# Splitting the mixer's weights during the first feed-forward of an encoder block, with both parts kept in DRAM

## The chip, the cores and the metric

The kernel runs on one core of a Trainium2 chip. The metric is the device time of one execution in microseconds (us); the time of a kernel is the median of several runs.

## What is computed

One encoder layer on 512 tokens of width 1024, in fp32, made of three sub-layers. Each one normalizes, modulates with a shift and a scale that come from a condition vector `c`, and adds its gated result to `x`:

```python
mod = (jax.nn.silu(c) @ w_ada[l] + b_ada[l]).reshape(B, N_MOD, D)
m = [mod[:, j] for j in range(N_MOD)]

h = modulate(rmsnorm(x, ffn1_pre_g[l]), m[0], m[1])
y = swiglu(h, ffn1_w_gate[l], ffn1_w_up[l], ffn1_w_down[l])
x = x + 0.5 * m[2][:, None, :] * rmsnorm(y, ffn1_post_g[l])

h = modulate(rmsnorm(x, mix_pre_g[l]), m[3], m[4])
proj = h @ w_in[l]
...
attn = dsa_attention(q, k, v, q_idx, k_idx, w_idx, rel_bias)
lru = rg_lru_branch(x_lru, g_lru, ...)
merged = jnp.concatenate([rmsnorm(attn, attn_out_g[l]), rmsnorm(lru, lru_out_g[l])], axis=-1)
y = merged @ w_out[l]
x = x + m[5][:, None, :] * rmsnorm(y, mix_post_g[l])
...
```

The third sub-layer is a feed-forward like the first. The hidden width of both is 2816. The mixer (the second sub-layer) projects `h` to queries, keys and values, to an indexer's queries, keys and weights, and to the recurrent branch's input and gate. The indexer scores all admissible keys of a query and keeps the best 128; attention runs over these alone. A gated linear recurrence runs beside it.

## The kernel before

**The product in three.** A weight is used in two parts: `hi`, the weight rounded to the matmul's fast fp32 form (`fp32r`), and `lo`, what is left over. The activations are split in the same way (`hhi`, `hlo`, and `ahi`, `alo` for the hidden layer). `product` (lines 261 to 269) does three matmuls for each of the (mostly 8) blocks of 128 input rows: hi by hi (L267), hi by the activation's lo (L268), lo by hi (L269). A weight piece is 128x1024 (512 KB, for 128 output columns) and takes 24 such matmuls of 512 tokens, or of 256 where the tokens are done in two halves.

**Weights.** The program is a list of items (`Item`), each with the weight pieces (`Load`) that it uses and an estimate of its time on TensorE (PE). `feed_dma` (L195) issues the next raw pieces on SP's queue into 3 raw buffers. `split` (L203) takes a place in a ring of 6 split pieces, makes `hi` by an ACT copy (L207) and `lo` by a subtraction (L209) on VectorE (DVE) or GpSimd (POOL), as the `Load` says. `feed` splits up to 4 pieces ahead of the item that runs. Pieces whose tokens are done in halves (`halves`, L244) keep 5 of the split pieces for the second half and load and split the others again. So the mixer's 33 pieces (21 of `w_in`, 4 of the value weights, 8 of `w_out`) are split 41 times, 14 of them with `lo` on DVE and 27 on POOL.

**Beside the items** run background tasks, which take a step when their share of the items' estimated time has passed (`tick`, L164). In the first feed-forward that is `mod_task` (L434): 14 groups of 512 modulation columns. Two 1 MB tiles of `w_ada` a group are loaded (`wa`, L443), DVE sums them over the input rows in 8 operations (`macc`, L429 and L431), and PE turns the sums into columns with four transposes (L465). DVE's and PE's queues are executed in order, so a transpose whose `macc` is late stops PE.

**The boundary** (L375) between two sub-layers adds the result to `X`, sums squares, and makes the next `h`; for each half of the tokens it is a chain through DVE, ACT, POOL and PE, which runs beside the products of the other half.

**The mixer** (L770 on) runs as items: ten pieces in token halves (`EARLY`), then whole pieces and attention steps in the order of the list `ORDER`. In the background DVE computes the indexer's scores (`scores`, L1020, sums at L1035), the best 128 by 16 rounds of MAX8 and MATCH_REPLACE8 (`top`, L1039, L1047 and L1048), and the recurrence (L1052 on; L1076, L1077, L1104, L1106, L1124, L1127). The tile `keys` is read by the score matmuls (L1027, L1028); the biases of attention (`bring`, L1150) are loaded into its place.

**Order.** A scheduler orders the instructions of ACT, DVE, POOL and PE by an estimate of the run at build time, PE at the start by hand. SP's DMA queue follows the program as written. `X`, the layer's input, is loaded at the start and stays in two blocks (`x0`, `x1`) until the boundary.

Of the kernel before, what the change touches and what calls it, by code (L numbers as in the profile page):

```python
# [2 lines left out]

F32 = mybir.dt.float32
F32R = mybir.dt.float32r
# [24 lines left out]

NSTART = 3
NHALF = 12

UNITS = [(i, g) for g in range(4) for i in range(2)] + [(i, g) for i in range(2, 4) for g in range(4)]

# [32 lines left out]
class Load:  # L68


    def __init__(self, src, shape, lo):
        self.src, self.shape, self.lo_eng = src, shape, lo
        self.uses = 0
        self.raw = self.hi = self.lo = None


class Item:
# [24 lines left out]
class Build:  # L102
    def __init__(self, tc, pools, ins, out):
        self.tc, self.nc = tc, tc.nc
        (self.const, self.blkp, self.ring, self.work, self.small, self.psum, self.dram) = pools
        self.i = ins
        self.out = out
        self.items = []
        self.bg = []
        self.pending = {}  # L110
        self.turn = 0
        self.mixed = False
        self.btemps = self.early = None


    def blk(self, name, slot, dtype=F32, shape=(P, 4, S)):
# [78 lines left out]
    def feed_dma(self):  # L195
        while self.nd < len(self.order) and self.waiting < RAW:
            l = self.order[self.nd]
            l.raw = self.ring.tile([P] + list(l.shape), F32, name="raw", tag="raw", bufs=RAW)
            self.nc.sync.dma_start(l.raw, l.src)
            self.nd += 1  # L200
            self.waiting += 1

    def split(self, l):  # L203
        nc = self.nc
        l.hi = self.ring.tile([P] + list(l.shape), F32R, name="hi", tag="hi", bufs=RING)
        l.lo = self.ring.tile([P] + list(l.shape), F32R, name="lo", tag="lo", bufs=RING)
        nc.scalar.activation(l.hi, l.raw, AF.Copy)  # L207
        eng = nc.gpsimd if l.lo_eng == "pool" else nc.vector
        eng.tensor_tensor(l.lo, l.raw, l.hi.bitcast(F32), op=ALU.subtract)  # L209
        self.alive += 1  # L210
        self.waiting -= 1
# [9 lines left out]
    def run(self):  # L221
        self.order, pos = [], {}
        for it in self.items:
            for l in it.loads:
                if id(l) not in pos:
                    pos[id(l)] = len(self.order)
                    self.order.append(l)
        self.nd = self.ns = self.alive = self.waiting = 0
        done = 0
        for it in self.items:  # L230
            if it.loads:
                done = max([done] + [pos[id(l)] for l in it.loads])
                self.feed(done + AHEAD)
            it.fn(*it.loads)
            for l in it.loads:
                l.uses -= 1
                if l.uses == 0:
                    self.alive -= 1
            self.tick(it.us)

    def add(self, us, fn, *loads):
        self.items.append(Item(us, fn, *loads))
# [417 lines left out]
    def ffn(self, w, a, gamma, beta, first):  # L660
# [10 lines left out]
        def gate_up(f, f0):  # L671
            def one(j):
                def fn(l):
                    new_act(f0)
                    ps = self.mm()
                    self.product(ps, l, self.h, FULL, range(8))
                    state[j] = ps
                    if j == 1:
                        self.act_tile(f - f0, state[0], state[1], FULL)
                return fn  # L680
            for j in range(2):
                lo = "pool" if first and f0 == 0 and j else "dve"
                self.add(5.2, one(j), Load(gu[f - (NSTART if first else 0), j], (8, P), lo))

        def gate_up_half(f, j, f0):
            def fn(l, half, tok):
# [20 lines left out]
        for t, (f0, f1) in enumerate(THIRDS):  # L707
            nf = f1 - f0
            fs = range(f0, f1)
            if t == 0 and first:  # L710
                def st():
                    new_act(0)
                    self.start()
                    self.add_bg(self.mod_task(), 0.75)
                    if self.early:
                        with self.tc.issue_after(self.late.ins):
                            self.early()
# [11 lines left out]
                    down(t, d, nf)  # L729
            else:  # L730
                def evac(ps, d, k, half, tok, st):
                    nc.vector.tensor_tensor(self.Y[d][:, tok], self.Y[d][:, tok], ps[:, :256], op=ALU.add)
                    self.square_one(st, k, self.Y[d][:, tok], nc.vector if k >= 6 else nc.gpsimd)
                    nc.scalar.activation(self.Y[d][:, tok], self.Y[d][:, tok], AF.Copy, scale=a()[:, d:d + 1])
# [42 lines left out]
class Mixer:  # L777
# [11 lines left out]
    def plan(self):  # L789
# [5 lines left out]
        names += [("k", j) for j in range(4)] + [("q", j) for j in range(4)]  # L795
        index = {n: k for k, n in enumerate(names)}

        def load(n, lo="pool"):
            return Load(win[index[n]], (8, P), lo)


        def half_piece(n):
            def fn(l, half, tok):
                if n == EARLY[0] and half == 0:
# [2 lines left out]
                b.product(ps[:, :256], l, b.h, tok, range(8))  # L807
                self.evac(n, ps[:, :256], half, tok)
            return fn
        first_half, second_half = b.halves(lambda k: load(EARLY[k], ("dve", "pool")[k % 2]),  # L810
                                           [half_piece(n) for n in EARLY], 2.6, "h")
        b.items += first_half + second_half

        def whole(n, bank=None):
# [2 lines left out]
                b.product(ps, l, b.h, FULL, range(8))  # L817
                self.evac(n, ps, 1, FULL)
            b.add(5.2, fn, load(n))
        wvs = [Load(wv[j], (2, S), "pool") for j in range(4)]  # L820

        def value_piece(t):
            def fn(*ls):
# [28 lines left out]

        def y(half):
            return lambda e: self.y[half][:, 2 * e:2 * e + 2]
        first_half, second_half = b.last_products(
            lambda d: Load(b.i["wout"][d], (8, P), ("dve", "pool")[d % 2]), lambda: self.mg,
            (range(4, 8), range(4)), 2.6, evac, y,
            lambda: b.m(5), lambda: b.m(7), lambda: b.m(6), ("a3", "a1", "w1", "x1"), key="mg", bank=("wo", "mm"))
        def unit(k):
# [504 lines left out]
```

## Time and profile before

| | us |
|---|---|
| median of 3 runs | 1103.34 |
| lowest, highest | 1098.99, 1109.67 |
| the profiled execution, its own time | 1096.75 |
| its span, first to last instruction | 1095.0 |
| PE busy | 1046.9 (96%) |
| DVE busy | 661.6 (60%) |
| ACT busy | 455.0 (42%) |
| POOL busy | 221.7 (20%) |

A matmul counts as busy while it waits in the pipeline too, so PE's 96% isn't PE at its peak. PEld is the weight loading, which lies beside the matmuls. PEclk is the granted clock of TensorE, 1.00 for 2.4 GHz and 0.50 for 1.2 GHz. In time, the first feed-forward lies at 60 to 410 us, the mixer at 410 to 690, the second feed-forward after that.

### The profile page before, as it was taken

How to read it: one execution, taken by the hardware profiler on the slowest of the kernel's cores; microseconds unless marked ns; L12 is line 12 of the kernel's file. 1: busy time of each engine (PE TensorE's matmuls, PEld its weight loads, DVE VectorE, ACT ScalarE, POOL GpSimd, SP SyncE). 2: the span in 40 equal slices, each digit the busy share in tenths (PEclk: the TensorE clock that was granted, in tenths of full speed). 3: DMA queues.
4: the chain of work that ended last, by engine and by line, in shares of the span. 5: the costliest groups of instructions: out<-in, count | busy, mean ns of one | idle time of the engine just before them, and what ended most of it. 6: DMA issues, size and time to landing. Idle time of an engine off the chain costs nothing.

```text
span 1095.0 us, 14915 instructions
## 1 busy us (share of the span) xinstructions
PE 1046.9 (96%) x5798; PEld 880.8 (80%) x5798; DVE 661.6 (60%) x1077; ACT 455.0 (42%) x752; POOL 221.7 (20%) x178
## 2 busy tenths in 40 slices
PE   8999999999999979999899999699999999999995
PEld 7688878888888979987576669599988888888894
DVE  5598789733333378799998575995432333333434
ACT  5552222322222465654666574554332222222352
POOL 0020000000001365551323342755000000000232
PEclk9999999999999989999999999799999999999997
DMA  9577778533333263440323351333433323333312
GB/s 366 223 282 279 278 291 315 205 92 116 97 96 97 78 206 124 163 131 19 116 82 121 98 173 45 118 113 100 154 96 116 92 85 94 116 96 97 97 40 77
DMA packets 43014, 152.80 MB, mean 140 GB/s; under 512 B 5160, under 2 KB 10536, under 8 KB 38336
## 3 DMA queue, kind: packets, MB, share of 16 engines
q1 hardware_dynamic: 40656, 145.46, 39.3%
q0 software_dynamic: 2288, 6.40, 1.8%
q8 instruction: 45, 0.74, 0.3%
q14 instruction: 25, 0.20, 0.1%
HBM read 147.62 MB, written 6.31 MB: 141 GB/s over the span
## 4 chain that ended last, share of the span: by engine, by line
PE 71%; DVE 19%; issue 3%; DMA 3%; ACT 2%; SPq 0%; POOL 0%; DVEq 0%; ACTq 0%; POOLq 0%
PE mm L268 14%; PE mm L267 14%; PE mm L269 14%; PE wo L268 7%; PE wo L269 7%; PE wo L267 7%; DVE idx L1048 2%; DVE lo L209 2%; DVE m L1047 2%; DMA wa<-in_wa_dram 2%; DVE idx L1035 2%; PE mm L1176 2%; PE mm L647 1%; PE aux L1213 1%; DVE arena L1106 1%
## 5 line engine op out<-in xcount | busy, mean ns | idle before, releaser
L207 ACT ACTIVATE hi<-raw 128x1024 fp32r<-128x1024 f32 (+2 forms) x192 | 197.7, 1031 | 418.8 <-PE mm L268 161.1
L209 POOL TENSOR_TENSOR lo<-raw,hi 128x1024 fp32r<-128x1024 f32 x50 | 123.7, 2474 | 740.4 <-ACT hi L207 680.3
L209 DVE TENSOR_TENSOR lo<-raw,hi 128x1024 fp32r<-128x1024 f32 (+2 forms) x142 | 169.1, 1192 | 149.6 <-ACT hi L207 148.3
L267 PE MATMUL mm<-hhi,hi 128*128 128x512 f32 (+1 forms) x600 | 211.0, 353 | 2.0 <-ACT hhi L335 1.8
L268 PE MATMUL mm<-hlo,hi 128*128 128x512 f32 (+1 forms) x600 | 210.1, 351 | 0.8 <-DVE hlo L345 0.8
L269 PE MATMUL mm<-hhi,lo 128*128 128x512 f32 (+1 forms) x600 | 209.6, 350 | 0.0
L267 PE MATMUL wo<-hhi,hi 128*128 128x512 f32 (+1 forms) x400 | 146.5, 366 | 1.7 <-ACT arena L932 1.7
L269 PE MATMUL wo<-hhi,lo 128*128 128x512 f32 (+1 forms) x400 | 144.7, 362 | 2.1 <-POOL lo L209 2.1
L268 PE MATMUL wo<-hlo,hi 128*128 128x512 f32 (+1 forms) x400 | 144.2, 360 | 0.0
L267 PEld LDWEIGHTS mm<-hhi,hi 128*128 128x128 f32 x600 | 115.0, 192 | 18.3 <-ACT hhi L335 3.0
L268 PEld LDWEIGHTS mm<-hlo,hi 128*128 128x128 f32 x600 | 114.4, 191 | 16.0 <-DVE hlo L345 1.9
L269 PEld LDWEIGHTS mm<-hhi,lo 128*128 128x128 f32 x600 | 114.5, 191 | 14.9 <-issue 0.5
L268 PE MATMUL mm<-alo,hi 128*128 128x256 f32 (+1 forms) x330 | 109.8, 333 | 0.0
L267 PE MATMUL mm<-ahi,hi 128*128 128x256 f32 (+1 forms) x330 | 109.7, 333 | 0.0
L269 PE MATMUL mm<-ahi,lo 128*128 128x256 f32 (+1 forms) x330 | 109.7, 333 | 0.0
L267 PEld LDWEIGHTS wo<-hhi,hi 128*128 128x128 f32 x400 | 76.8, 192 | 14.3 <-ACT arena L932 2.1
L269 PEld LDWEIGHTS wo<-hhi,lo 128*128 128x128 f32 x400 | 76.2, 191 | 14.1 <-POOL lo L209 2.6
L268 PEld LDWEIGHTS wo<-hlo,hi 128*128 128x128 f32 x400 | 76.3, 191 | 11.7 <-issue 1.0
L431 DVE SCALAR_TENSOR_TENSOR macc<-wa,cs,macc 128x512 f32<-128x512 f32 x98 | 74.8, 764 | 10.2 <-DMA wa<-in_wa_dram 8.9
L268 PEld LDWEIGHTS mm<-alo,hi 128*128 128x128 f32 x330 | 62.7, 190 | 6.1
L269 PEld LDWEIGHTS mm<-ahi,lo 128*128 128x128 f32 x330 | 62.7, 190 | 5.9
L267 PEld LDWEIGHTS mm<-ahi,hi 128*128 128x128 f32 x330 | 62.5, 190 | 6.0
(258 smaller groups left out, 1617.5 us busy)
## 6 DMA issues: line engine op xcount, KB each, us to landing
raw<-in_gu_dram SPq DMA_DIRECT2D x89, 512.0 KB, 3.5
wa<-in_wa_dram SPq DMA_DIRECT2D x36, 1024.0 KB, 6.0
raw<-in_dn_dram SPq DMA_DIRECT2D x32, 448.0 KB, 3.4
raw<-in_win_dram SPq DMA_DIRECT2D x26, 512.0 KB, 3.6
raw<-in_dn_dram SPq DMA_DIRECT2D x22, 512.0 KB, 3.5
raw<-in_wout_dram SPq DMA_DIRECT2D x11, 512.0 KB, 3.9
raw<-in_w_dram SPq DMA_DIRECT2D x8, 384.0 KB, 10.2
X<-in_x_dram SPq DMA_DIRECT2D x4, 512.0 KB, 6.1
```

The costliest lines, as they stand in the source:

```text
L207: nc.scalar.activation(l.hi, l.raw, AF.Copy)
L209: eng.tensor_tensor(l.lo, l.raw, l.hi.bitcast(F32), op=ALU.subtract)
L267: self.nc.tensor.matmul(ps, l.hi[:, kt], xh[kt][:, tok], start=(q == 0), stop=False)
L268: self.nc.tensor.matmul(ps, l.hi[:, kt], xl[kt][:, tok], start=False, stop=False)
L269: self.nc.tensor.matmul(ps, l.lo[:, kt], xh[kt][:, tok], start=False, stop=(q == n - 1))
L431: nc.vector.scalar_tensor_tensor(acc, w[:, k], ck, acc, op0=ALU.mult, op1=ALU.add)
L647: self.nc.tensor.matmul(ps, w[:, j], x[k], start=(k == 0 and part == 0), stop=(k == ND - 1 and part == 2))
L1035: nc.vector.scalar_tensor_tensor(sc, rl[:, :n], w, sc, op0=ALU.mult, op1=ALU.add)
L1047: nc.vector.max(out=m8, in_=src)
L1048: nc.vector.match_replace(out=wk, in_to_replace=m8, in_values=src, imm_value=NEG)
L1106: nc.vector.scalar_tensor_tensor(xc[:, t:], x[:, :S - t], b.col("convw", 4 * (3 - t) + j), xc[:, t:], op0=ALU.mult, op1=ALU.add)
L1176: nc.tensor.matmul(ps[:, :n], self.q[rows, g, i * P:(i + 1) * P], self.k[rows, g, :n], start=True, stop=False)
```

## The change

A new class `Pre` stands for a piece that is split once, ahead of time. `pre` gives each of the 33 mixer pieces two DRAM tiles, and a background task `presplit` does the splits during the first feed-forward, one about every 7.4 us of the items' estimated time. It works in the blocks `x0` and `x1`, whose input has been used by then: it loads a raw piece, forms `hi` beside it on ACT, overwrites the raw piece with `lo` on DVE, and stores both to DRAM. All its DMAs are on POOL's queue (33 loads, 66 stores). When it has ended, `X` is loaded again from the input in DRAM. The task is run to its end before the first half-token result of the last products of the first feed-forward.

A `Load` that has a `Pre` skips the raw buffers and the split: `split` takes the place in the ring and issues two 512 KB DMAs on SP's queue, one for each part (82 in all, for 41 places). Four low parts at the beginning of the first feed-forward, which POOL formed, go to DVE.

```diff
@@ class Load / Pre
+    def __init__(self, src, shape, lo, pre=None):
+        self.src, self.shape, self.lo_eng, self.pre = src, shape, lo, pre
...
@@ feed_dma
             l = self.order[self.nd]
+            if l.pre:
+                self.nd += 1
+                continue
@@ split
+        if l.pre:
+            for t, part in zip((l.hi, l.lo), l.pre.parts):
+                nc.sync.dma_start(t.bitcast(F32), part)
+            self.alive += 1
+            return
@@ new
+    def pre(self, src, shape):
+        return Pre(src, shape, [self.dram.tile([P] + list(shape), F32, name=f"pre{next(self.count)}") for _ in range(2)])
+
+    def presplit(self):
+        nc = self.nc
+        at = {}
+        def fetch(k):
+            if k < len(self.pres):
+                t = at[k] = self.blk("pre", XS[k % 2], shape=[P, 2] + list(self.pres[k].shape))
+                nc.gpsimd.dma_start(t[:, 0], self.pres[k].src)
+        fetch(0)
+        fetch(1)
+        yield PACE
+        for k, p in enumerate(self.pres):
+            t = at.pop(k)
+            raw, hi = t[:, 0], t[:, 1].bitcast(F32R)
+            nc.scalar.activation(hi, raw, AF.Copy)
+            nc.vector.tensor_tensor(raw.bitcast(F32R), raw, t[:, 1], op=ALU.subtract)
+            nc.gpsimd.dma_start(p.parts[0], t[:, 1])
+            nc.gpsimd.dma_start(p.parts[1], raw)
+            fetch(k + 2)
+            yield PACE
+        self.X = self.big("X", XS)
+        for q in range(4):
+            nc.gpsimd.dma_start(self.X.tiles[q // 2][:, 2 * (q % 2):2 * (q % 2) + 2], self.i["x"][:, 2 * q:2 * q + 2])
@@ gate_up (first feed-forward)
-                lo = "pool" if first and f0 == 0 and j else "dve"
-                self.add(5.2, one(j), Load(gu[f - (NSTART if first else 0), j], (8, P), lo))
+                self.add(5.2, one(j), Load(gu[f - (NSTART if first else 0), j], (8, P), "dve"))
@@ start item, and first result of the last products
                     self.add_bg(self.mod_task(), 0.75)
+                    self.presplit_ = self.add_bg(self.presplit())
...
+                    if k == half == 0 and first:
+                        self.drain(self.presplit_)
@@ mixer
+        pres = {n: b.pre(win[k], (8, P)) for n, k in index.items()}
...
-        wvs = [Load(wv[j], (2, S), "pool") for j in range(4)]
+        wvs = [Load(wv[j], (2, S), None, b.pre(wv[j], (2, S))) for j in range(4)]
```

**DVE in the first feed-forward.** One group of modulation sums before, from its first operation to that of the next group: two weight pieces (`lo`) are split between the sums, and the columns of the group ahead are reduced (`modc`).

```order
L429 TENSOR_SCALAR macc<-wa,cs 128x512
L431 SCALAR_TENSOR_TENSOR macc<-wa,cs,macc 128x512 x2
L209 TENSOR_TENSOR lo<-raw,hi 128x1024
L431 SCALAR_TENSOR_TENSOR macc<-wa,cs,macc 128x512 x2
L466 TENSOR_REDUCE modc<-aux 128x4
L431 SCALAR_TENSOR_TENSOR macc<-wa,cs,macc 128x512 x2
L655 TENSOR_TENSOR a<-wo,sg 128x512
L431 SCALAR_TENSOR_TENSOR macc<-wa,cs,macc 128x512
L209 TENSOR_TENSOR lo<-raw,hi 128x1024
L658 TENSOR_TENSOR alo_1319<-a,ahi_1317 128x512
```

A group of the changed kernel. L480 and L482 are the sums, L230 is the low part, and L283 is a presplit piece.

```order
L480 TENSOR_SCALAR macc<-wa,cs 128x512
L709 TENSOR_TENSOR alo_1449<-a,ahi_1447 128x512
L525 TENSOR_TENSOR modc<-modc,cols 128x8
L482 SCALAR_TENSOR_TENSOR macc<-wa,cs,macc 128x512 x5
L230 TENSOR_TENSOR lo<-raw,hi 128x1024
L482 SCALAR_TENSOR_TENSOR macc<-wa,cs,macc 128x512
L230 TENSOR_TENSOR lo<-raw,hi 128x1024
L482 SCALAR_TENSOR_TENSOR macc<-wa,cs,macc 128x512
L283 TENSOR_TENSOR pre<-pre 128x1024
L706 TENSOR_TENSOR a<-mm,sg 128x512
```

Each group now has one presplit piece (two in one of them). On PE the last group's transposes stand behind 712 products of `product` where they stood behind 608, the first group's behind 98 where they stood behind 72.

**POOL in the mixer.** Before, between the boundary's `h` and the first scaled attention weights (`lgs`), and behind these:

```order
L336 TENSOR_SCALAR h_3627<-u,modc 128x256 x2
L209 TENSOR_TENSOR lo<-raw,hi 128x1024 x12
L1185 TENSOR_SCALAR lgs<-lgs,mx 128x128 x2
L1185 TENSOR_SCALAR lgs<-lgs,mx 128x256 x2
L209 TENSOR_TENSOR lo<-raw,hi 128x1024 x6
```

The same place now (L387 is the boundary's `h`, L1241 the scaling, L899 the load of `X` from its copy in DRAM):

```order
L387 TENSOR_SCALAR h_3875<-u,modc 128x256 x2
L1241 TENSOR_SCALAR lgs<-lgs,mx 128x128 x2
L1241 TENSOR_SCALAR lgs<-lgs,mx 128x256 x2
L899 DMA X_5698<-xd 128x4x256 x2
L1241 TENSOR_SCALAR lgs<-lgs,mx 128x128 x2
```

The 18 subtractions are gone from this stretch of POOL's queue.

**SP's queue around the first bias loads.** Before, the raw data of ten projection pieces, of the four value pieces (`wv`) and of three further projection pieces, then the biases:

```order
L199 DMA raw<-in_win_dram 128x1024 x10
L199 DMA raw<-in_wv_dram 128x1024 x4
L199 DMA raw<-in_win_dram 128x1024 x3
L1150 DMA bring<-skew 128x2x128
L1150 DMA bring<-skew 128x2x256
```

Now, from the last value piece (pre_125 and pre_126 are its two parts; pre_93 and pre_94 are those of the next projection piece, the second gate piece of the recurrent branch):

```order
L225 DMA hi<-pre_125 128x1024
L225 DMA lo<-pre_126 128x1024
L1206 DMA bring<-skew 128x2x128
L1206 DMA bring<-skew 128x2x256
L1206 DMA bring<-skew 128x2x128
L225 DMA hi<-pre_93 128x1024
L225 DMA lo<-pre_94 128x1024
```

The projection pieces behind the value pieces are now issued behind the first three bias loads. On PE the last score matmuls (L1027, L1028) stood behind the products of that second gate piece; they now stand ahead of them.

## Rows read from the trace of the kernel before

**Rows 1.** The page: the chain that ended last, by engine.

```profile
PE 71%; DVE 19%; issue 3%; DMA 3%; ACT 2%; SPq 0%; POOL 0%; DVEq 0%; ACTq 0%; POOLq 0%
```

**Rows 2.** Busy times in stretches, us; columns in the first row.

```profile
core 0: us, PE busy (x) PEld busy (x) DVE busy (x) ACT busy (x) POOL busy (x), PEclk, DMA share, GB/s
50.00:205.00 155.00, 152.88 (x693) 124.58 (x693) 136.62 (x218) 51.85 (x68) 9.64 (x4) 1.00 0.78 287
205.00:345.00 140.00, 140.00 (x621) 115.97 (x620) 51.73 (x58) 38.05 (x47) 2.96 (x2) 1.00 0.32 100
400.00:455.00 55.00, 46.66 (x342) 44.05 (x341) 40.60 (x49) 29.33 (x59) 34.01 (x31) 0.91 0.46 157
475.00:600.00 125.00, 117.35 (x519) 88.75 (x518) 120.54 (x268) 71.78 (x123) 40.16 (x26) 0.97 0.29 92
675.00:750.00 75.00, 63.48 (x491) 60.53 (x490) 66.90 (x90) 42.22 (x74) 44.40 (x31) 0.91 0.33 106
800.00:825.00 25.00, 25.00 (x112) 20.72 (x111) 6.97 (x6) 9.06 (x12) 0.00 (x0) 1.00 0.33 106
```

**Rows 3.** The timeline from 484 to 489 us: start, us, engine, what.

```profile
483.98 2.40 POOL L209 TENSOR_TENSOR lo<-raw,hi 128x1024 fp32r<-128x1024 f32 x1 [0.80 <-ACT hi L207]
...
484.06 2.74 DVE L1035 SCALAR_TENSOR_TENSOR idx<-rl,wcol,idx 128x384 f32<-128x384 f32 x1
...
488.55 0.60 DVE L1035 SCALAR_TENSOR_TENSOR idx<-rl,wcol,idx 128x384 f32<-128x384 f32 x1
```

**Rows 4.** DVE by shape, 475 to 600 us: count, busy, mean ns, idle.

```profile
L1035 DVE SCALAR_TENSOR_TENSOR idx<-rl,wcol,idx 128x384 f32<-128x384 f32 x7 | 7.7, 1093 | 0.0
L1106 DVE SCALAR_TENSOR_TENSOR arena<-arena,cols 128x509 f32<-128x509 f32 x4 | 6.9, 1730 | 0.0
L1035 DVE SCALAR_TENSOR_TENSOR idx<-rl,wcol,idx 128x512 f32<-128x512 f32 x7 | 6.6, 945 | 0.0
L1127 DVE SCALAR_TENSOR_TENSOR arena<-g,arena 128x512 f32<-128x512 f32 x4 | 6.5, 1628 | 0.0
...
L1077 DVE SCALAR_TENSOR_TENSOR lru<-arena 128x512 f32<-128x512 f32 x4 | 4.3, 1079 | 0.0
...
L209 DVE TENSOR_TENSOR lo<-raw,hi 128x1024 fp32r<-128x1024 f32 x3 | 3.7, 1221 | 1.7 <-ACT hi L207 1.7
...
L1106 DVE SCALAR_TENSOR_TENSOR arena<-arena,cols 128x511 f32<-128x511 f32 x4 | 2.9, 735 | 0.0
```

**Rows 5.** The tile keys: readers, ns min/median/max, first and last start.

```profile
L1028 PE MATMUL aux<-keys,qi x24: 280/338/397, 453.3 to 518.6; 128*128 128x256 f32 x8, 128*128 128x384 f32 x8, 128*128 128x512 f32 x8
```

**Rows 6.** SP's queue, timeline: start, us until the last is issued, what.

```profile
519.07 1.41 SPq L1150 DMA_DIRECT2D bring<-skew  x3
```

**Rows 7.** The page: DMA issues, count, KB each, median us to landing.

```profile
raw<-in_win_dram SPq DMA_DIRECT2D x26, 512.0 KB, 3.6
```

**Rows 8.** The chain in order of time, 385 to 465 us: start, us, what.

```profile
400.89 3.19 DVE lo L209
...
420.82 1.16 DVE lo L209
...
434.20 1.14 DVE lo L209
```

**Rows 9.** PE, timeline: start, us, what, idle before and its releaser.

```profile
127.47 0.63 PE L465 MATMUL aux<-ident,macc 128*128 128x128 f32 x4 [0.19 <-DVE macc L431]
```

**Rows 10.** The tile wa, 48 to 215 us: its operations, waits, landings.

```profile
L431 DVE SCALAR_TENSOR_TENSOR macc<-wa,cs,macc x98: 734/751/2307, 63.0 to 205.6; 128x512 f32<-128x512 f32 x98
...
  DMA wa<-in_wa_dram: 14.0, 13
...
DMA to landing us min/median/max: 4.7/5.1/10.9
```

**Rows 11.** DMA from 48 to 206 us: rate in 40 equal slices, and packets.

```profile
GB/s 202 212 315 403 226 296 66 354 351 274 288 137 284 430 122 416 278 203 199 197 392 295 201 342 417 203 374 237 249 415 272 423 272 364 267 193 421 214 355 234
DMA packets 8507, 45.01 MB, mean 285 GB/s; under 512 B 951, under 2 KB 951, under 8 KB 4912
```

More of the change, by code (lines that the diff above doesn't have):

```diff
@@ L1 @@
+import itertools
 import concourse.bass as bass
@@ L32 @@
 NHALF = 12
+PACE = 7.4
 UNITS = [(i, g) for g in range(4) for i in range(2)] + [(i, g) for i in range(2, 4) for g in range(4)]
@@ L68, with __init__ @@
 class Load:
-    def __init__(self, src, shape, lo):
-        self.src, self.shape, self.lo_eng = src, shape, lo
+    def __init__(self, src, shape, lo, pre=None):
+        self.src, self.shape, self.lo_eng, self.pre = src, shape, lo, pre
         self.uses = 0
         self.raw = self.hi = self.lo = None
+class Pre:
+    def __init__(self, src, shape, parts):
+        self.src, self.shape, self.parts = src, shape, parts
 class Item:
@@ L113, in __init__ @@
         self.btemps = self.early = None
+        self.count = itertools.count()
     def blk(self, name, slot, dtype=F32, shape=(P, 4, S)):
@@ L228, in run @@
         self.nd = self.ns = self.alive = self.waiting = 0
+        self.pres = list(dict.fromkeys(l.pre for l in self.order if l.pre))
         done = 0
@@ L796, in plan, with load @@
         index = {n: k for k, n in enumerate(names)}
-        def load(n, lo="pool"):
-            return Load(win[index[n]], (8, P), lo)
+        pres = {n: b.pre(win[k], (8, P)) for n, k in index.items()}
+        def load(n):
+            return Load(win[index[n]], (8, P), None, pres[n])
         def half_piece(n):
@@ L809, in half_piece @@
             return fn
-        first_half, second_half = b.halves(lambda k: load(EARLY[k], ("dve", "pool")[k % 2]),
+        first_half, second_half = b.halves(lambda k: load(EARLY[k]),
                                            [half_piece(n) for n in EARLY], 2.6, "h")
@@ L854, in y @@
             return lambda e: self.y[half][:, 2 * e:2 * e + 2]
+        pouts = [b.pre(b.i["wout"][d], (8, P)) for d in range(ND)]
         first_half, second_half = b.last_products(
-            lambda d: Load(b.i["wout"][d], (8, P), ("dve", "pool")[d % 2]), lambda: self.mg,
+            lambda d: Load(b.i["wout"][d], (8, P), None, pouts[d]), lambda: self.mg,
             (range(4, 8), range(4)), 2.6, evac, y,
```

## The prediction

> **What bounds the kernel now.** I read the chain of waits first, then the busy times by stage, then the waits inside the stages in which TensorE (PE) is not full. The chain is PE for 71% and VectorE (DVE) for 19% [rows 1]: a kernel bound by matmuls, with places where DVE ends last. Where they are is seen by stage [rows 2]. From 800 us on, PE starts 112 products of 512 columns in 25 us (0.223 us each) with the weight loads busy 20.72 of 25. From 400 to 455 (the boundary into the mixer) PE is idle for 8.3 us and the granted clock averages 0.91 of 2.4 GHz, another 5 us. From 475 to 600 DVE is busy 120.54 of 125 us, and the weight loads 88.75: at the full-speed ratio of 20.72 to 25 that is 107 us of PE work spread over 125. From 675 to 750 PE is idle for 11.5 us and the clock is 0.91 again. The first feed-forward looks full (152.88 of 155 us), but DVE is busy for 136.62 of those 155 us and the DMA engines for 78%.
>
> So there are two questions. What does the mixer give back when its 41 splits are gone, and has the first feed-forward room for 33 splits and 52 MB of traffic?
>
> **What goes from the mixer.** Before, 14 of the 41 low parts are formed on DVE and 27 on POOL, and each piece needs one ACT copy. The POOL ones cost DVE as well: while POOL subtracted at 483.98 (2.40 us), a DVE operation that started 0.08 us later took 2.74 us; the same line and shape takes 0.60 us at 488.55, when POOL is quiet [rows 3]. The groups of 475 to 600 show how often this strikes [rows 4]. Line 1035 with 384 elements: 7 x (1.093 - 0.60) = 3.4 us. With 512 elements, against the 0.735 us that line 1106 takes undisturbed: 7 x (0.945 - 0.735) = 1.5. Line 1106 with 509 elements: 4 x (1.730 - 0.735) = 4.0. Lines 1127 and 1077, against the same 0.735: 4 x 0.893 + 4 x 0.344 = 4.9. That is 13.8 us, a low count since other forms are stretched too. With the three low parts on DVE (3.7 us) it makes 17.5 us less DVE work in a stage where DVE ends last. PE needs 107 of these 125 us, so at most 18 us can come back.
>
> Against this stands a new wait. SP's queue is in program order. Before, the raw data of the three pieces behind the value pieces was issued ahead of the first bias loads. Now the two parts of each piece are issued when a ring slot is taken, and the first of these (second gate piece, pre_93) stands behind three bias loads. These wait until the last index score has read the tile that they overwrite: the last score matmul starts at 518.6 us, the bias loads are issued at 519.07 and hold SP for 1.41 us [rows 5, 6]. A piece of 512 KB lands 3.6 us after its issue [rows 7]. PE can't start that piece until 0.5 + 1.4 + 0.4 + 3.6 = 6 us after the last score, where before it worked on it in the meantime. DVE has the top-k of the second half to do by then, so I count 5 us of it. Stage 475 to 600: -18 + 5 = **-13 us**; bounds 0 (all of it eaten by the wait or by PE) and -18.
>
> Boundary into the mixer: in the chain, three low parts of mixer pieces stand between the squares and PE's next product for the first half and three for the second; one of them, at 400.89, took 3.19 us beside a POOL subtraction, the others 1.16 and 1.14 [rows 8]. That is 3.19 + 5 x 1.15 = 9 us of a chain in which PE waits for 8.3 us; some is hidden by the other operations of the boundary. I take **-6 us**; bounds 0 and -11 (the sum and 2 us of the clock). Boundary out of the mixer: only three late pieces of the output product are split there, some 3 us. I take **-2**; bounds 0 and -4. The pieces now bring 1 MB each where 0.5 MB came; from 475 to 600 the engines move 92 GB/s [rows 2], so the doubled loads have room there and I put nothing down.
>
> **What comes into the first feed-forward.** 33 pieces: an ACT copy, a DVE subtraction (1.22 us, [rows 4]), one load and two stores of 512 KB from POOL's queue. After 205 us DVE is busy for 51.73 of 140 us and the DMA engines for 32% [rows 2]: 16 or so of the pieces fall there and hide. The stretch before is the matter, where the 14 groups of modulation columns (macc) run on DVE. Each group's columns are turned by four transposes in PE's in-order queue, so PE waits when a group is late. At 127.47 us it does: the transpose starts 0.19 us after it could, released by macc [rows 9]. The groups are thus already the pace of this stretch: the accumulations start from 63.0 to 205.6 us, 10.2 us a group, of which DVE sits 14.0 us in 13 waits for the next weights, 1 us a group [rows 10].
>
> The new order moves PE's transposes back: the last stands behind 712 products of lines 267 to 269 instead of 608, so that PE reaches one every 47 products, 47 x 0.223 + 0.5 = 11.0 us, and it reaches the first some 4 us late. The new group of DVE: 10.2 + 1.2 (one presplit piece) = 11.4 us if the waits stay, 10.4 if they vanish under it. DMA: 59.8 MB between the first and the last group (26 weight tiles of 1.05 MB, 24 raw pieces of 0.5, 13 presplit pieces of 1.57), 4.6 MB a group. The best twentieths of the stretch move 415 to 430 GB/s, the mean is 285 [rows 11]: at 423 a group takes 10.9 us, so the engines would be full almost throughout. A weight tile lands 5.1 us after its issue [rows 10], of which 1.05 MB at 423 is 2.5 us; if the second queue takes half of the engines all the while it lands 2.5 us later. A group then lies between 11.0 and 10.2 + 1.2 + 2.5 = 13.9 us. I take 11.8, near the DVE end, since the presplit pieces are two at a time and leave gaps. PE's loss: 13 x (11.8 - 11.0) - 4 = **+6.4 us**; bounds 0 and 13 x 2.9 - 4 = +34.
>
> The "HBM Reference" page of the Trainium skill (Specifications) gives an effective 358 GB/s per core, and more for a core that streams alone. By 358 a group would take 12.8 us and the loss would be 20 us, which would cancel the gain; the trace's slices of 415 to 430 GB/s [rows 11] speak against that figure here.
>
> Small ends: two presplit operations stand in the start's DVE and ACT order, about 1 us each, and four low parts of the first pieces move from POOL to DVE; I add **+1.5**, bounds -2 (a POOL subtraction beside the start goes) and +4. The input is fetched again before the boundary, behind the last stores, 40 us ahead of its use: nothing.
>
> **Sum.** -13 - 6 - 2 + 6.4 + 1.5 = -13 us. The profiled execution took 1096.75 us (span 1095.0 and 1.75 around it), at the low end of three runs with a median of 1103.34. I put the sum on the middle of the two, 1100: **1087 us**. About 1% (11 us) is what a measurement of this kernel can tell from no change.
>
> **Rivals.**
> A: the first feed-forward becomes DMA-bound, and the kernel slower. For it: 4.6 MB a group against 285 GB/s today, and weights that already land just in time [rows 10, 11]. Against it: presplit traffic has slack of its own, and PE's order leaves 11.0 us a group. It decides from a group of 12.8 us, where 13 x 1.8 - 4 = 19.4 eats the gain; at the bound of 13.9 the loss is 34 us and the time 1100 - 21 + 34 + 1.5 = 1114. The page "DMA: Bandwidth & Descriptors" (Issuing engines are not separate DMA queues) says that POOL's transfers share the same 16 engines as SP's, so a second queue brings no bandwidth; by that rule the 4.6 MB a group stand as counted, and this rival keeps its chance.
> B: the mixer gives little back. The relief on DVE is taken by the wait for pre_93 and by attention's latencies, and the boundary by its own reductions: -5 - 3 in place of -21, so 1100 - 8 + 6.4 + 1.5 = 1100. For it: DVE's in-order queue meets late gate pieces; against it: rows 3 show the stretch on the bounding engine itself.
> C: no cost at all in the feed-forward and the whole of the mixer's gain, 1100 - 33 (18, 11 and 4, the far bounds) = 1067. It belongs to the forecast's side.
>
> **How the numbers follow.** Forecast (with C's side) 0.55, A 0.23, B 0.22. Faster by over 1%: 0.49, nearly all of the forecast; slower by over 1%: 0.20 (most of A); within 1%: 0.31 (B, the mild part of A, the edge of the forecast). The forecast's own range is 1068 to 1094; with B and nearly all of A it is 1068 to 1112.
>
> **What would show it.** In the profile after: POOL without subtractions from 455 to 600, line 1035's mean for 384 elements near 0.6 us, and that stage near 112 us. The macc groups every 11 to 12 us, the waits of PE's transposes for macc under 10 us in all. A gap of about 5 us on PE behind the last index score. I am wrong if weight tiles land after 8 us or more and the groups take 13 (A), or if DVE has idle time in the mixer and PE still isn't faster (B).

## The result, and the profile after

The changed kernel took 1119.53 us (median of 4 runs, 1117.38 to 1119.96), the kernel before 1101.42 (4 runs, 1098.99 to 1109.67): a ratio of 1.0149, interval 1.0109 to 1.019. It is slower by 18 us where 13 us less were forecast, and lies outside the forecast's range (1068 to 1094) and outside the wider one with the rivals (to 1112).

The page's chain by engine, to be held against [rows 1]:

```profile
PE 62%; issue 18%; DMA 9%; DVE 4%; POOL 3%; ACT 2%; SPq 0%; DVEq 0%; POOLq 0%; ACTq 0%
```

PE has lost 9 points of the path, DVE 15. In their place stand "issue" and DMA: the chain now runs through POOL's presplit transfers. The same stretches as in [rows 2], up to 600 us:

```profile
core 0: us, PE busy (x) PEld busy (x) DVE busy (x) ACT busy (x) POOL busy (x), PEclk, DMA share, GB/s
50.00:205.00 155.00, 144.36 (x629) 116.61 (x628) 120.70 (x188) 58.44 (x73) 19.20 (x37) 0.97 0.92 343
205.00:345.00 140.00, 131.07 (x558) 106.23 (x557) 85.58 (x106) 49.07 (x55) 22.83 (x43) 0.95 0.89 312
400.00:455.00 55.00, 51.72 (x414) 51.14 (x414) 28.45 (x45) 26.99 (x55) 23.46 (x22) 0.97 0.57 212
475.00:600.00 125.00, 120.21 (x637) 100.34 (x636) 109.51 (x259) 62.09 (x110) 7.11 (x11) 0.99 0.51 184
```

From 50 to 205 us the DMA share rises from 0.78 to 0.92 and the rate from 287 to 343 GB/s; PE loses 8.5 us there and 9 more from 205 to 345, where it had been full. Since later stretches are shifted in time, I also count products: the start of the n-th matmul of `product`'s three lines (267 to 269 before, 318 to 320 after), read from both traces.

| product | before, us | after, us | later by |
|---|---|---|---|
| 0 | 62.2 | 61.5 | -0.7 |
| 360 | 148.8 | 145.7 | -3.1 |
| 480 | 178.6 | 186.3 | 7.7 |
| 720 | 234.5 | 263.0 | 28.5 |
| 1260 | 355.6 | 384.1 | 28.5 |
| 1320 | 362.8 | 400.9 | 38.1 |
| 1620 | 399.4 | 438.0 | 38.6 |
| 1860 | 444.3 | 475.3 | 31.0 |
| 2520 | 665.7 | 687.0 | 21.3 |
| 3000 | 743.0 | 765.2 | 22.2 |

So the first feed-forward costs 38 us, in two places: 31.6 us between products 360 and 720, and 9.6 between 1260 and 1320. The mixer gives 17 back.

**The first place.** How long transfers took from 50 to 205 us (issues, KB each, median us to landing), after and then before:

```profile
wa<-in_wa_dram SPq DMA_DIRECT2D x22, 1024.0 KB, 6.3
pre<-pre POOLq DMA_DIRECT2D x24, 512.0 KB, 8.1
raw<-in_gu_dram SPq DMA_DIRECT2D x16, 512.0 KB, 8.7
pre<-in_win_dram POOLq DMA_DIRECT2D x11, 512.0 KB, 8.2
```

```profile
wa<-in_wa_dram SPq DMA_DIRECT2D x28, 1024.0 KB, 5.1
raw<-in_gu_dram SPq DMA_DIRECT2D x18, 512.0 KB, 6.0
```

A raw piece of the feed-forward lands 8.7 us after its issue instead of 6.0. What that does is seen in the timeline around one of PE's stops (start, us, engine, what, and in brackets the idle time and what ended it):

```profile
155.42 5.41 SPq L494 DMA_DIRECT2D wa<-in_wa_dram  x2
...
160.92 1.54 SPq L215 DMA_DIRECT2D raw<-in_gu_dram  x2
...
169.74 1.06 ACT L228 ACTIVATE hi<-raw 128x1024 fp32r<-128x1024 f32 x1 [1.91 <-DMA raw<-in_gu_dram]
...
170.85 0.79 PE L318 MATMUL mm<-hhi,hi 128*128 128x512 f32 x1 [3.66 <-ACT hi L228]
```

SP holds the next two raw pieces behind two weight tiles, which it can issue only when the sums have read the tiles before them and their blocks are free. The raw pieces go out at 160.92, the first is there for ACT at 169.74, and PE starts at 170.85 after 3.66 us of idling. PE's waits from 150 to 250 us name the same two links:

```profile
PE mm L318 <- ACT hi L228: 11.5, 4, 3.7
PE mm L320 <- DVE lo L230: 4.4, 3, 2.2
```

The transposes of the modulation sums, which I had expected to stop PE, are not in that list. They stop DVE instead. DVE reduces the transposed columns in order between its sums, and the first line is its wait for PE's transposes (40 to 400 us; before, it had none). The second is SP's wait for the sums to free the blocks of the weight tiles (150 to 262 us):

```profile
DVE modc L517 <- PE aux L516: 23.1, 12, 4.4
SPq L494 <- DVE macc L482: 79.1, 14, 10.0
```

So the waits form a ring: a late raw piece delays PE, PE's next transposes delay DVE's sums, the sums delay the weight tiles, and the raw pieces stand behind the tiles.

The groups themselves (the tile wa from 48 to 262 us, as in [rows 10]):

```profile
L482 DVE SCALAR_TENSOR_TENSOR macc<-wa,cs,macc x98: 740/752/754, 70.8 to 255.1; 128x512 f32<-128x512 f32 x98
...
  DMA wa<-in_wa_dram: 2.2, 2
```

They take 70.8 to 255.1 us, by the reckoning of the prediction 184.3 / 14 = 13.2 us a group, where it was 10.2 and 11.8 was forecast. DVE now waits only 2.2 us for weight tiles: late tiles were not what slowed it. By these waits a group is 10.2 + 1.2 (the presplit piece) - 1.0 + 0.2 (the waits for tiles, before and after) + 1.7 (for the transposes, 23.1 / 14) = 12.3 us; the other 0.9 us I did not trace.

**The second place.** The chain at the end of the first feed-forward:

```profile
378.00 3.77 DMA pre<-in_wout_dram
...
381.87 1.07 ACT pre L282
...
384.10 1.23 DVE lo L230
...
385.35 5.76 DMA raw<-in_dn_dram
...
391.19 1.06 ACT hi L228
...
392.80 2.46 DVE alo L709
...
395.30 0.58 PE mm L319
```

A presplit piece arrives at 381.8. Its ACT copy stands in the in-order queue ahead of the copies that PE needs, and its DVE subtraction ahead of the low part at 384.10. A raw buffer comes free only with that low part, and its next piece takes 5.76 us to land. ACT's waits from 345 to 395 us show that this is the rule there, 24.1 us for five presplit loads:

```profile
ACT pre L282 <- DMA pre<-in_wout_dram: 24.1, 5, 5.9
```

**The mixer.** Line 1091 (1035 before), line 1162 (1106) and line 1183 (1127) from 475 to 620 us:

```profile
L1091 DVE SCALAR_TENSOR_TENSOR idx<-rl,wcol,idx 128x384 f32<-128x384 f32 x7 | 4.3, 618 | 1.3 <-ACT rl L1086 1.3
...
L1162 DVE SCALAR_TENSOR_TENSOR arena<-arena,cols 128x509 f32<-128x509 f32 x4 | 3.0, 740 | 0.0
...
L1183 DVE SCALAR_TENSOR_TENSOR arena<-g,arena 128x512 f32<-128x512 f32 x4 | 2.7, 680 | 0.5 <-ACT g L1182 0.5
```

Against [rows 4] their means fall from 1093 to 618, from 1730 to 740 and from 1628 to 680 ns: undisturbed values throughout. Behind the last index score stands the new wait:

```profile
541.17 0.39 PE L1084 MATMUL aux<-keys,qi 128*128 128x512 f32 x1
...
541.64 1.39 SPq L1206 DMA_DIRECT2D bring<-skew  x3
...
543.08 0.47 SPq L225 DMA_DIRECT2D hi<-pre  x1
...
547.37 0.50 PE L318 MATMUL wo<-hhi,hi 128*128 128x512 f32 x1 [3.28 <-DMA hi<-pre]
```

From the last score (541.17) to the piece that was queued behind the bias loads it is 6.2 us; the prediction's terms made 6.

### The profile page after: what moved, and what is told of

Read it like the earlier page. It is cut to its first block, busy times and chain, and to the rows that moved or that the text cites. A ratio compares the mean times of both kernels' runs of the same rounds, so it can differ in the third digit from the quotient of the medians.

```text
span 1117.2 us, 15192 instructions
## 1 busy us (share of the span) xinstructions
PE 1055.8 (95%) x5798; PEld 886.8 (79%) x5798; DVE 649.2 (58%) x1100; ACT 452.0 (40%) x744; POOL 200.1 (18%) x250
## 3 DMA queue, kind: packets, MB, share of 16 engines
q0 software_dynamic: 17120, 60.41, 15.3%
## 4 chain that ended last, share of the span: by engine, by line
PE 62%; issue 18%; DMA 9%; DVE 4%; POOL 3%; ACT 2%; SPq 0%; DVEq 0%; POOLq 0%; ACTq 0%
PE mm L319 10%; PE mm L320 10%; PE mm L318 10%; PE wo L320 7%; PE wo L318 7%; PE wo L319 7%; DMA pre<-pre 5%; PE mm L1232 2%; DMA pre<-in_win_dram 2%; PE aux L1269 1%; DMA wa<-in_wa_dram 1%; POOL pre L275 1%; PE mm L1252 1%; PE mm L698 1%; DMA pre<-in_wout_dram 1%
## 5 line engine op out<-in xcount | busy, mean ns | idle before, releaser
L228 ACT ACTIVATE hi<-raw 128x1024 fp32r<-128x1024 f32 (+2 forms) x151 | 153.9, 1023 | 276.9 <-PE mm L319 106.8
L318 PE MATMUL mm<-hhi,hi 128*128 128x512 f32 (+1 forms) x600 | 213.7, 357 | 14.3 <-ACT hi L228 11.5
L230 DVE TENSOR_TENSOR lo<-raw,hi 128x1024 fp32r<-128x1024 f32 (+2 forms) x132 | 156.8, 1190 | 120.9 <-ACT hi L228 120.0
L320 PE MATMUL mm<-hhi,lo 128*128 128x512 f32 (+1 forms) x600 | 214.2, 357 | 4.4 <-DVE lo L230 4.4
L319 PE MATMUL mm<-hlo,hi 128*128 128x512 f32 (+1 forms) x600 | 213.7, 357 | 1.7 <-DVE hlo L396 1.7
L320 PEld LDWEIGHTS mm<-hhi,lo 128*128 128x128 f32 x600 | 116.4, 194 | 22.2 <-DVE lo L230 6.6
L230 POOL TENSOR_TENSOR lo<-raw,hi 128x1024 fp32r<-128x1024 f32 x19 | 48.3, 2543 | 318.4 <-ACT hi L228 311.9
L482 DVE SCALAR_TENSOR_TENSOR macc<-wa,cs,macc 128x512 f32<-128x512 f32 x98 | 73.4, 749 | 4.2 <-DMA wa<-in_wa_dram 2.2
L283 DVE TENSOR_TENSOR pre<-pre 128x1024 fp32r<-128x1024 f32 x33 | 40.3, 1221 | 48.9 <-ACT pre L282 48.9
```

The costliest lines, as they stand in the source:

```text
L283: nc.vector.tensor_tensor(raw.bitcast(F32R), raw, t[:, 1], op=ALU.subtract)
L318: self.nc.tensor.matmul(ps, l.hi[:, kt], xh[kt][:, tok], start=(q == 0), stop=False)
L319: self.nc.tensor.matmul(ps, l.hi[:, kt], xl[kt][:, tok], start=False, stop=False)
L320: self.nc.tensor.matmul(ps, l.lo[:, kt], xh[kt][:, tok], start=False, stop=(q == n - 1))
L482: nc.vector.scalar_tensor_tensor(acc, w[:, k], ck, acc, op0=ALU.mult, op1=ALU.add)
```

## The experiments

Ratios are to runs of the kernel before that shared the chip (medians of 1101.4 to 1101.8 us). "Later by" is in us against the profiled run of the kernel before, at the products of the table above. That profiled run (1096.75 us) is 4.7 us below the median, so these columns show each gain smaller than the medians do, by about that much where a version's own profiled run lies at its median (e6's lies 3.6 us below).

| run | median, us | ratio (95%) | 720 | 1320 | 1860 | 2520 |
|---|---|---|---|---|---|---|
| changed kernel | 1119.5 | 1.0149 (1.0109 to 1.019) | 28.5 | 38.1 | 31.0 | 21.3 |
| e1_nopre | 1081.1 | 0.9818 (0.9793 to 0.9842) | 0.1 | 0.1 | -6.2 | -14.5 |
| e2_smallstores | 1094.1 | 0.9938 (0.9916 to 0.996) | 11.9 | 11.9 | 6.0 | -2.5 |
| e3_noops | 1113.1 | 1.0106 (1.0067 to 1.0145) | 28.4 | 28.4 | 22.3 | 17.5 |
| e4_late25 | 1080.5 | 0.9816 (0.9795 to 0.9838) | -0.8 | -0.8 | -7.0 | -15.3 |
| e5_late25_bias | 1072.9 | 0.9748 (0.9724 to 0.9772) | -3.3 | -3.3 | -10.3 | -25.1 |
| e6_late25_two | 1099.0 | 0.9977 (0.9952 to 1.0002) | -3.3 | 14.7 | 7.7 | -1.3 |
| e7_after25 | 1110.5 | 1.0081 (1.0061 to 1.0102) | 27.0 | 27.0 | 19.9 | 11.2 |
| e8_late33 | 1111.1 | 1.0094 (1.0068 to 1.0119) | -1.6 | -1.6 | 32.5 | 15.0 |
| e9_lo_act | 1084.7 | 0.9845 (0.9827 to 0.9862) | 2.4 | 2.4 | -1.9 | -13.2 |
| e10_lo_dve | 1097.5 | 0.996 (0.9936 to 0.9985) | 1.0 | 1.0 | -2.4 | -0.4 |
| e11_mid25 | 1076.4 | 0.9783 (0.975 to 0.9815) | -2.4 | 5.5 | -1.4 | -16.3 |

**e1: no presplit.**

```diff
-        self.pres = list(dict.fromkeys(l.pre for l in self.order if l.pre))
+        self.pres = list(dict.fromkeys(l.pre for l in self.order if l.pre))[:2]
...
-            for t, part in zip((l.hi, l.lo), l.pre.parts):
+            for t, part in zip((l.hi, l.lo), self.pres[self.ns % 2].parts):
```

> Only the first two mixer pieces are split ahead of time; all 41 part loads read the parts of these two, so the mixer does the same loads and products with wrong weights and the first feed-forward is left almost as before. It separates the mixer's gain from the first feed-forward's loss. Theory D (the loss of the changed kernel sits in the first feed-forward, the mixer itself gained 17 us): product 1260 within 3 us of the kernel before, 1101 - 17 = 1084 us. Rival M (the mixer's gain was only slack that the late start gave back, such as loads that had more time): 1095 to 1103 us.

The first feed-forward is that of before (0.1 us at product 1320), and the mixer gains 20 us by the medians, 15 by the trace. Theory D holds: the gain is real, and the loss sits in the first feed-forward.

**e2: small stores; e3: no operations.** e2 has e1's second edit and these stores; e3 leaves out the copy and the subtraction from the third piece on and stores the raw block twice.

```diff
-            nc.gpsimd.dma_start(p.parts[0], t[:, 1])
-            nc.gpsimd.dma_start(p.parts[1], raw)
+            nc.gpsimd.dma_start(*((p.parts[0], t[:, 1]) if k < 2 else (p.parts[0][:, 0], t[:, 1, 0])))
+            nc.gpsimd.dma_start(*((p.parts[1], raw) if k < 2 else (p.parts[1][:, 0], raw[:, 0])))
```

> The presplit task with all its loads, ACT and DVE operations and waits, but from the third piece on each store writes 64 KB in place of 512 KB; the mixer's part loads read the parts of the first two pieces (wrong weights, same traffic). Theory D (transfers: the stores and loads fill the DMA engines, so raw pieces land late): the loss at product 720, 28.5 us in the changed kernel, falls to 5 us or less, and the stall at the end of the first feed-forward (9.6 us) shrinks since a slot comes round faster; 1084 to 1092 us. Rival O (orders: presplit operations in the in-order queues of ACT and DVE, PE's transposes behind more products): the loss at product 720 stays above 20 us; 1108 to 1120 us.

> The presplit task with all its loads and full stores, but without the ACT copy and the DVE subtraction from the third piece on (the raw block is stored twice; the mixer's part loads read the parts of the first two pieces, wrong weights, same traffic). Theory D: the loss at product 720 stays above 20 us, the stall at the end goes; 1105 to 1115 us. Rival O: the loss at product 720 falls to 5 us or less; 1084 to 1090 us.

e3 has a loss of the same size at product 720 (28.4 us) without the ACT and DVE work, so that work is not needed for it; the loss at the end goes. The two kernels differ in more than that work: without the operations the presplit runs faster and moves more, 385 GB/s where it was 343. And it leaves half of rival O untouched, as the last of PE's transposes still stands behind 716 products. By the traces it stands behind 706 in e2, which loses 11.9, and behind 708 in e11 (below), which loses nothing at product 720: that order alone is not the cause. e2 falls to 11.9 and not to 5 or less: with smaller stores a piece comes round sooner, 18 presplit loads are issued from 50 to 205 us in place of 13, and the DMA engines are as busy as in the changed kernel (the value pieces' stores are also larger than intended, 256 KB; stretches 50 to 205 and 205 to 345 us of e2, columns as above):

```profile
50.00:205.00 155.00, 154.66 (x703) 127.30 (x703) 135.70 (x211) 67.76 (x84) 28.43 (x52) 1.00 0.91 342
205.00:345.00 140.00, 132.12 (x572) 107.50 (x571) 81.53 (x97) 50.80 (x59) 25.41 (x47) 0.96 0.65 225
```

In e3 the engines are never idle, and still no more than 385 GB/s passes (50 to 205 us):

```profile
50.00:205.00 155.00, 142.94 (x625) 115.53 (x624) 108.38 (x175) 46.35 (x61) 26.15 (x49) 0.97 1.00 385
```

There PE's longest waits are for the sums, the link that I had expected in the changed kernel:

```profile
PE aux L517 <- DVE macc L483: 13.1, 3, 5.8
PE mm L319 <- ACT hi L228: 5.3, 5, 2.5
```

Which link breaks depends on the order of the work. That one breaks goes with the presplit's traffic beside the modulation, but how much is lost doesn't follow from its amount: e2 and the changed kernel have the same rate and share from 50 to 205 us, and lose 11.9 and 28.5 us.

**e4: a late start, four blocks, 25 pieces.**

```diff
+PS = ("x0", "x1", "w0", "w1")
...
-                t = at[k] = self.blk("pre", XS[k % 2], shape=[P, 2] + list(self.pres[k].shape))
+                t = at[k] = self.blk("pre", PS[k % len(PS)], shape=[P, 2] + list(self.pres[k].shape))
+                if k < len(PS):
+                    with self.tc.issue_after(self.gate.ins):
+                        nc.vector.memset(t[:, 0, 0, :1], 0.0)
```

`gate` is the last operation of the modulation sums. The memset is ordered behind it, and the first load of each block waits for the memset's column. `PACE` is 6.5, and the output pieces have no `Pre`.

> A full version: the presplit of the 25 projection and value pieces begins when the last modulation sum is done (a one-column memset behind it holds the first loads back), in four blocks (the two of the input and the two of the modulation weights) in place of two; the eight output pieces are split in the mixer as before. Theory D: no loss up to product 720, 25 x 1.57 MB = 39 MB and some 18 MB of the feed-forward's own in 180 us, 317 GB/s, just under what the engines move; stall at the end 0 to 10 us; 1084 to 1095 us. Rival O (in-order queues): the loss moves to the second half of the first feed-forward, 15 to 25 us there; 1100 to 1112 us.

1080.5 us, as good as no presplit at all: nothing is lost at product 720 or 1320. Yet the DMA engines are as busy as they were in the changed kernel beside the modulation (205 to 345 us):

```profile
205.00:345.00 140.00, 140.00 (x621) 115.89 (x620) 78.69 (x85) 60.97 (x70) 43.18 (x74) 1.00 0.92 355
```

A share of 0.92 does no harm here. In this stretch no weight tiles stand ahead of the raw pieces, and no sums and transposes in the queues of DVE and PE; which of these matters was not tried by itself. What is left is the wait for the second gate piece:

```profile
510.70 0.79 PE L322 MATMUL wo<-hhi,hi 128*128 128x512 f32 x1 [4.64 <-DMA hi<-pre]
```

**e5: the bias loads on POOL's queue.**

```diff
-        self.nc.sync.dma_start(self.bring[u], self.skew[2 * g:2 * g + 2, :, S - n:].rearrange("h p j -> p h j"))
+        self.nc.gpsimd.dma_start(self.bring[u], self.skew[2 * g:2 * g + 2, :, S - n:].rearrange("h p j -> p h j"))
```

> The late version of 25 pieces with the bias loads on POOL's queue in place of SP's, so that the second gate piece is no longer queued behind three bias loads that wait for the last index score. In the late version PE stood 4.9 us at that place (505.47 to 510.70 us). Theory W (that wait is the queue's order): the gap falls under 1 us and the time to 1080.5 - 4.9 = 1075 to 1077 us. Rival (PE meets the next late thing, DVE's top-k or the attention's biases, now on a slower queue): 1079 to 1083 us.

The gap is gone, and PE is busy throughout from 475 to 600 us:

```profile
475.00:600.00 125.00, 125.00 (x581) 91.42 (x580) 107.34 (x285) 75.89 (x155) 33.74 (x46) 1.00 0.45 152
```

At 1072.9 us this is the fastest version, 2.5% below the kernel before and 4.2% below the changed one; 7.6 us came where 4.9 were expected.

**e6: two blocks.** As e4, with `PS = ("x0", "x1")`.

> The late version of 25 pieces with two blocks in place of four. In the changed kernel a piece took about 8.3 us in its two blocks from 262 to 382 us, with the modulation done. Theory S (two blocks set the pace of the presplit by the round trip of load, split and store): 25 x 7.5 to 8.3 us is 188 to 208 us, 8 to 28 us longer than there is, and PE's products at the end of the first feed-forward wait in the in-order queues of ACT and DVE: 1086 to 1105 us. Rival (only the start after the modulation matters): 1079 to 1083 us.

1099.0 us. The 25 copies run from 208.4 to 379.5 us, 7.1 us each:

```profile
L286 ACT ACTIVATE pre<-pre x25: 1045/1060/1063, 208.4 to 379.5; 128x1024 fp32r<-128x1024 f32 x25
```

They end inside the half-token products, as in the changed kernel, and PE waits there:

```profile
PE mm L322 <- ACT ahi L714: 10.5, 2, 6.9
```

**e7: the changed kernel without the output pieces.** Only `pouts[d]` and its list are taken out; the pieces are split in the mixer as before.

> The changed kernel without the eight output pieces (split in the mixer as before), with its early start and two blocks: the presplit then ends at about 316 us, long before the boundary. Theory E (the 9.6 us lost between products 1260 and 1320 is the presplit running late into the half-token products): that loss goes and the one of 28.5 us before stays; 1119.5 - 9.6 + 0 to 2 = 1110 to 1112 us. Rival (the end's loss is the reload of X and the boundary itself): 1117 to 1121 us.

1110.5 us, and nothing is lost between products 1260 and 1320: the second place is the presplit's late end, and the first place is untouched (27.0).

**e8: all 33 pieces late.** e5 with the output pieces, `PACE = 5.0`.

> The late version with the bias loads on POOL's queue (1072.9 us with 25 pieces), now with all 33 pieces. Theory B (what the DMA engines can move sets the limit): 33 x 1.57 MB = 52 MB and 18 MB of the feed-forward's own at the 372 GB/s that its stretches show when full (287 GB/s at a share of 0.78) take 188 us where there are some 175, so PE loses 8 to 15 us at the end of the first feed-forward, and the output pieces, whose low parts the boundary out of the mixer hardly waits for, give back 0 to 2: 1078 to 1088 us. Rival (there is room, and the output pieces gain as the others did): 1066 to 1072 us.

1111.1 us: the sign was right, the size was not, by either theory. The loss isn't in the products but behind them: X's blocks hold the last pieces, so X comes back late and the boundary stands for 38.5 us. The chain there, and the wait on PE:

```profile
388.61 13.41 DMA pre<-pre
...
415.93 6.78 DMA pre<-pre
...
425.86 4.73 DMA X<-in_x_dram
...
437.89 1.13 PE aux L347 x4
```

```profile
PE aux L347 <- POOL ssum L411: 38.5, 1, 38.5
```

**e9: the low parts on ACT.** The kernel before; where a low part was formed on POOL in the mixer:

```diff
+            nc.scalar.activation(l.lo, l.raw, AF.Copy)
```

> The kernel before, with the 27 POOL subtractions of the mixer replaced by a second ACT copy (the low part is then wrong), so POOL is quiet and DVE has no more work than before. Theory L (each POOL subtraction stretches a DVE operation beside it, and DVE sets the pace from 475 to 600 us): line 1035 with 384 elements falls from 1.09 to 0.6 us, the stage gives back 8 to 14 us, 1088 to 1094 us. Rival (the stretched operations cost nothing, something else sets the pace there): 1098 to 1103 us.

1084.7 us, 17 us less, beyond the range of theory L. The lines of [rows 4] fall to the same values as in the changed kernel (475 to 600 us; lines 1040, 1111 and 1132 are 1035, 1106 and 1127):

```profile
L1040 DVE SCALAR_TENSOR_TENSOR idx<-rl,wcol,idx 128x384 f32<-128x384 f32 x5 | 3.1, 613 | 1.3 <-ACT rl L1035 1.2
...
L1111 DVE SCALAR_TENSOR_TENSOR arena<-arena,cols 128x509 f32<-128x509 f32 x4 | 3.0, 740 | 0.0
...
L1132 DVE SCALAR_TENSOR_TENSOR arena<-g,arena 128x512 f32<-128x512 f32 x4 | 2.8, 690 | 1.7 <-ACT g L1131 1.7
```

Taking POOL's subtractions away gives 17 of the mixer's 20 us, with every split still in place. The low parts also come sooner from ACT than from POOL; in the kernel before PE waited only 2.1 us for POOL's low parts, so most of the gain is not that.

**e10: the low parts on DVE.** The kernel before with "dve" for every "pool" of the mixer's pieces.

> The kernel before with the 27 POOL subtractions of the mixer on DVE, nothing in DRAM. With an ACT copy in their place the time was 1084.7 us, so their cost to DVE was 17 us of the path. Theory L: each costs DVE 1.22 us itself in place of some 1.75 us of stretching, and DVE sets the pace in part of the mixer only: 1088 to 1098 us. Rival (27 x 1.22 = 33 us more in DVE's in-order queue, ahead of sums and top-k, cancels the gain): 1100 to 1110 us.

1097.5 us in 10 runs (1090.6 to 1102.5), at the edge of theory L's range. In its profile it is 20 us ahead at product 2400 and has lost that by 2520. PE idles for 4.3 us from 580 to 600, and from 600 to 620 us its clock was granted at half (1.2 GHz), which takes up to 10 us more; the rest of that loss I didn't trace:

```profile
580.00:600.00 20.00, 15.73 (x80) 10.75 (x80) 19.37 (x74) 11.17 (x32) 4.97 (x11) 0.90 0.30 103
600.00:610.00 10.00, 10.00 (x34) 4.31 (x33) 5.05 (x19) 4.37 (x17) 2.06 (x4) 0.50 0.13 42
610.00:620.00 10.00, 10.00 (x28) 5.23 (x28) 3.12 (x14) 2.48 (x8) 1.62 (x3) 0.50 0.14 39
```

**e11: start in the middle.** e5 with `gate` behind the seventh group of sums and two blocks.

> The 25 pieces from the middle of the modulation on (behind the seventh of 14 groups of sums, near 137 us), in two blocks, with the bias loads on POOL's queue; 6 pieces then stand among the modulation sums, 19 behind them, at 7.1 us each 135 us, so they end in time. Theory D by bytes (each piece of 1.57 MB among the modulation sums costs PE its share of the 28.5 us, 13 pieces in the changed kernel, 2.2 us each): 1072.9 + 13 = 1084 to 1089 us. Rival R (reserve: the changed kernel lost nothing until 150 us, 90 us after its first piece, as the pieces loaded ahead and PE's lead were used up first; 70 us of overload are borne by it): 1072 to 1077 us.

1076.4 us. The pieces that stand among the sums cost nothing at product 720, as rival R has it, though the engines are as full as in the changed kernel and the last sum starts only at 223.5 us:

```profile
137.00:225.00 88.00, 88.00 (x402) 72.77 (x401) 72.31 (x101) 31.16 (x38) 11.36 (x21) 1.00 0.92 359
```

So 88 us of such traffic beside the sums are borne; that a reserve is used up in that time, as rival R says, is argued and not shown. The 7.9 us that are lost at product 1320 lie where e6 lost with two blocks.

## Why the prediction was wrong

1. **The first feed-forward (+6.4 forecast, 38.1 found) is where it failed**, at the step "I take 11.8, near the DVE end". The group took 13.2 us, near the upper bound; the same formula then gives 13 x (13.2 - 11.0) - 4 = +24.6, against 28.5 found at product 720. Behind the choice stood a price for the traffic: "at 423 a group takes 10.9 us", taken from the best slices of the stretch [rows 11], which last 4 us each. The row for the whole stretch [rows 2] had the price: 287 GB/s at a share of 0.78 is 368 at a share of 1. After, 343 at 0.92 is 373, and e3 moved 385 at 1.00. At 370 the 4.6 MB of a group take 12.4 us, above the 11.0 that PE's order leaves. But the price alone doesn't turn the sign: with 12.4 the formula gives 13 x 1.4 - 4 = +14, and the sum -5.

The prediction also put a wait at nothing. It let PE wait for DVE's sums, but never DVE for PE's transposes, which the new order had moved back behind more products; DVE then stood 23.1 us there, 1.7 us a group. Rival A had the place and the size (a loss of 34, with +1.5 and a full gain 1114), but only one of its two signs came: the groups took 13 us, while weight tiles landed after 6.3 us in the median, not 8. The link was another: I expected late weight tiles and PE waiting at the transposes; the raw pieces were late, behind the tiles in SP's queue, and DVE waited at the transposes. How much of the 13.2 is the order of the queues, and how much traffic alone, was not tried and stays open.

The "HBM Reference" page of the Trainium skill (Specifications) gives 358 GB/s per core, and about 425 for a core that streams alone; I set the first figure aside for the slices of 415 to 430. The stretches show 343 at a share of 0.92 and 385 at 1.00, so the first was nearer than mine, though not a ceiling.

2. **"16 or so of the pieces fall there and hide"**: 16 did fall behind the sums, but not all were hidden. In two blocks a piece took 8.3 us (16 ACT copies of line 282 from 256.8 to 381.9 us), so the last were split among the half-token products; that is the 9.6 us (gone in e7, and found by itself in e6). The prediction had priced the operations of a piece and not its round trip.

3. **The mixer (-21 forecast)** was right: 20 us by e1's median (15 by its trace), 17.3 between products 1620 and 2520 of the changed kernel's trace. POOL's subtractions were the mechanism (e9). By parts, boundary in: -6 forecast, 38.6 to 31.0, -7.6 found. Stage and what follows it to product 2520: -13 forecast, -9.7 found in the changed kernel, -14.8 in e5, where the wait for the gate piece is gone: that wait was forecast at 5, and PE stood 3.3 us for the high part and 0.9 for the low one. Boundary out: -2 forecast, +0.9 found: taking the splits of its three late pieces away gave nothing. The parts missed by up to 3 us each, partly in opposite directions.

4. **The start (+1.5)**: -0.7, nothing.

Rival B falls with e1. Rival C's 1067, the mixer's gain without the feed-forward's loss, is what e4 and e5 come near to once the start is moved.

## What to carry to other kernels

The rate that a stretch can sustain was nearer to its mean rate divided by the DMA share of the same row than to the best slices of the rate curve: 368 GB/s before, 346 to 390 in the rows with the presplit beside the modulation (the changed kernel, e2, e3, e11), where single slices reached 430. The quotient belongs to a row of the same kind of traffic: at a share of 0.32 it was 312 [rows 2]. A price for the bytes is not enough where in-order queues wait for each other in a ring; then a delay on one engine comes back through the others. Work that is moved into idle DMA time needs a stretch where the transfers that others wait for have slack, and its own round trip (load, compute, store) divided by its number of blocks has to fit: 33 pieces at 8.3 us did not, 25 in four blocks behind the modulation did. Before work is moved through DRAM at all, it is worth finding which part of it hurts: here the subtractions on POOL beside DVE were 17 of the 20 us.

## What the runs showed of the hardware

A stop of PE cost more than its length here. After the wait of 2.2 us at 157.7 the granted clock from 159.8 to 163.4 us was 0.56, near the level of 1.2 GHz, and matmuls started 0.43 us apart in place of 0.227. In e10 idling of 4.3 us was followed by 20 us at 0.50.

The share of the DMA engines says less than it seems to: 0.92 went with a loss of 28 us beside the modulation, and with none in e11's 88 us beside the modulation or in e4's stretch behind it. And the DVE operations beside a POOL subtraction returned to their own times as soon as POOL was quiet, 740 ns for 1730, in the changed kernel and in e9 alike. The "SBUF — State Buffer" page of the Trainium skill (Terms) describes a port pair of DVE and GpSimd which one of them holds for a whole instruction; e9's rows agree in that DVE's delay goes with POOL's subtraction, and no run here shows that the port is the reason.
